# First weight pieces halved, first piece on ScalarE's queue, two x parts split on VectorE, other warm-up sizes

## The chip, the cores and the metric

The kernel runs on one core of a Trainium2 chip. Its time is the device time of one execution in microseconds; lower is better. Five engines work side by side, each through its own list of instructions in order: TensorE (PE, matmuls), VectorE (DVE), ScalarE (ACT), GpSimd (POOL) and SyncE (SP, which here only issues DMA transfers). ScalarE and GpSimd can issue transfers too.

## The reference

Two transformer blocks in a row on one sequence of 256 tokens of width 1024, all in float32. The part that matters here is the very beginning of the first block:

```python
xn = rms_norm(x, norm1_w[l])
z = xn @ w_in[l]
(q, k_c, v_c, k_s, v_s, k_w, v_w, g_nsa, xr, gr, g_a, g_b) = jnp.split(z, IN_SPLITS, axis=-1)
# rms_norm: xf * rsqrt(mean(xf * xf) + EPS) * w
```

After it come sparse attention with compressed keys, a gated linear recurrence (its decay uses `softplus(-lam)`), a merge, an MLP, and a second block with gated feed-forward layers and two more kinds of attention. All of that is matmuls with weights that are read once from memory, some 170 MB in all.

## The kernel before, in words

Precision: each float32 operand is split into a high part in TensorE's faster float32 format and a low part, the rest. A product takes three matmuls (high x high, high x low, low x high; `mmx`, L296 to L300). A weight piece is split by ScalarE (high: a copy, L248) and VectorE (low: a subtraction, L249). The activations of a norm are split in the same way by `split2` (L325 to L333), multiplied there by the norm's weight; the norm's 1/rms per token is applied later, when a product is taken out of PSUM.

Weights: `Plan` packs the weight blocks of all steps, in the order of the steps, into pieces. The first four pieces have 512 columns (256 KB), all others up to 1024 (512 KB). The first six pieces are loaded one by one (`chunks`, `load_to`), the later ones two to a transfer. The first `EARLY` transfers take tiles of the pool of 12 large buffers, the later ones three tiles of their own. `split_to` splits pieces two ahead of the one that is wanted, into five buffers for the high and five for the low parts.

The start: `setup` (L428) writes a tile of ones, runs three float32 matmuls on it as a warm-up (six passes in the profile, tile `hot`), loads the table for the sigmoid, and issues the first loads: the vector of small weights (`vec`, 56 KB) from ScalarE's queue, and from SyncE's queue x parts 0 to 1, weight piece 0, x parts 2 to 4, piece 1, x parts 5 to 7, piece 2. Then it splits the eight parts of x (tile `u`), high on ScalarE (L332), low on VectorE (L333).

The first projection is `kcvc` (step kv0, `fm1`): eight parts k of x by 256 columns, two blocks of three matmuls for each k, 48 matmuls of 256 columns. So pieces 0 to 3 hold k = 0 and 1, 2 and 3, 4 and 5, 6 and 7. The projection q0 follows (pieces 4 and 5), then xr0, k0, q1, xr1. Step `norm` (`norm0`, L542) squares x on ScalarE (L550), ordered behind the high part of piece 5, adds the squares on VectorE, and runs a short chain for 1/rms: sums on TensorE (L495), VectorE (L466), a power on GpSimd (tile `rs_A`, L468), a broadcast by TensorE (tile `bc_A`, L502), ScalarE (`rb_A`, L504). The evacuations of kcvc, q, xr and k multiply by `rb_A`.

Step `prep` (`rnn_prep`, L881) works out softplus of the recurrence's lambda, on 8 columns: two small operations, two sigmoids on ScalarE, and then a long row of GpSimd operations (L890 to L904). Its result is used only in the recurrence, later.

Order: the steps are issued in the order written in `ORDER_1`, but a scheduler then lays down each engine's list from an estimated timeline: an engine takes, of the instructions that are ready by that estimate, the one issued first (or marked as of high priority, as the norm's chain is). So work of later steps moves ahead where an engine is idle in the estimate: `prep` is begun as soon as `vec` is there. `behind` adds an order between two instructions of one engine and no wait. A transfer waits before its issue until the one eight places before it has landed.

Of the kernel before, what the change touches and what calls it, by code (L numbers as in the profile page):

```python
# [8 lines left out]
F32 = mybir.dt.float32  # L9
F32R = mybir.dt.float32r  # L10
AF = mybir.ActivationFunctionType
ALU = mybir.AluOpType
AX = mybir.AxisListType

P = 128
# [5 lines left out]
EPS = 1e-6  # L21
LOW = -float(2.0 ** 100)
PIECE = 1024
EARLY = 6
WIDE = ("g", "g", "g", "s", "s", "o")


# [1 line left out]
class Plan:  # L29
# [6 lines left out]

    def add(self, key, name, rows, cols):
        w = sum(n for _, n in cols)
        room = PIECE if len(self.pieces) > 4 else PIECE // 2
        if self.fresh or not self.pieces or self.pieces[-1][0] + w > room:  # L40
            self.pieces.append([0, []])
            self.fresh = False
        p = self.pieces[-1]
        self.loc[key] = (len(self.pieces) - 1, p[0], w)
        p[1].append((name, rows, cols))
        p[0] += w
# [4 lines left out]
    def chunks(self):  # L51

        out, i, n = [], 0, len(self.pieces)
        while i < n:
            c = 1 if i < 6 else 2
            out.append(list(range(i, min(n, i + c))))
            i += c
        return out
# [130 lines left out]
class Prog:  # L189
# [15 lines left out]
    def prepare(self):  # L205
        self.chunks = self.plan.chunks()
        self.chunk_of = {}
        self.off = []
        o = 0
        for ci, ch in enumerate(self.chunks):  # L210
            w = sum(self.plan.pieces[i][0] for i in ch)
            self.off.append((o, w))
            o += P * w
            x = 0
            for i in ch:
                self.chunk_of[i] = (ci, x)
                x += self.plan.pieces[i][0]
        self.total = o
        self.raw = {}
        self.split = {}  # L220
        self.n_dma = 0
        self.n_split = 0
        self.hi_ins = []
        self.raw_ins = []

    def load_to(self, c):
        while self.n_dma <= min(c, len(self.chunks) - 1):
            ci = self.n_dma
            o, w = self.off[ci]
            pool = "big" if ci < EARLY else "raw"  # L230
            t = self.pools[pool].tile([P, 2 * PIECE], F32, tag=pool, name=f"raw{ci}")
            self.raw_ins.append(self.nc.sync.dma_start(out=t[:, :w], in_=self.d["ws"][o:o + P * w].rearrange("(p w) -> p w", p=P)))
            if ci:
                self.behind(*self.raw_ins[:-3:-1])
            self.raw[ci] = t
            self.n_dma += 1

    def split_to(self, i):
        nc = self.nc
        while self.n_split <= min(i, len(self.plan.pieces) - 1):  # L240
            p = self.n_split
            ci, x = self.chunk_of[p]
            self.load_to(ci + 2 if ci >= EARLY else max(ci + 2, EARLY))
            w = self.plan.pieces[p][0]
            src = self.raw[ci][:, x:x + w]
            hi = self.pools["whi"].tile([P, PIECE], F32R, tag="whi", name=f"whi{p}")
            lo = self.pools["wlo"].tile([P, PIECE], F32R, tag="wlo", name=f"wlo{p}")
            self.hi_ins.append(nc.scalar.activation(out=hi[:, :w], in_=src, func=AF.Copy))  # L248
            nc.vector.tensor_tensor(out=lo[:, :w], in0=src, in1=hi[:, :w].bitcast(F32), op=ALU.subtract)  # L249
            self.split[p] = (hi, lo)  # L250
            self.n_split += 1

# [122 lines left out]
def build(nc, tc, d, out, es, dbg=None):  # L375
# [22 lines left out]
    G = Prog(nc, tc, pools, d, dbg)  # L398
    one = pools["one"]
    V = {}  # L400
    S = {}

    def keep(name, shape, dt=F32):
        t = one.tile(list(shape), dt, tag=name, name=name)
        S[name] = t
        return t
# [21 lines left out]
    def setup():  # L428

        hot = G.tmp("hot")  # L430
        nc.vector.memset(hot, 1.0)
        hb = G.ps("t", "hot")
        for _ in range(3):
            nc.tensor.matmul(hb, hot[:, :P], hot, start=True, stop=True)
        warm = G.small((P, 1), "warm")
        nc.vector.memset(warm, 1.0)
        nc.scalar.activation(out=warm, in_=warm, func=AF.Sigmoid)
        ones = keep("ones", (P, 2))
        nc.vector.memset(ones, 1.0)
        nc.vector.memset(keep("mhalf", (P, 2)), -0.5)  # L440
        res = G.big("res")
        S["res"] = res
        vec = keep("vec", (P, NVEC))
        nc.scalar.dma_start(out=vec, in_=d["vec"])
        nc.sync.dma_start(out=res[:, 0:2, :], in_=d["x"][:, 0:2, :])
        G.load_to(0)
        nc.sync.dma_start(out=res[:, 2:5, :], in_=d["x"][:, 2:5, :])
        G.load_to(1)
        nc.sync.dma_start(out=res[:, 5:8, :], in_=d["x"][:, 5:8, :])
        G.load_to(2)  # L450
        vec2 = keep("vec2", (P, NVEC2))
        o = 0
        for k in _VEC:
            V[k] = vec[:, o:o + 8]
            o += 8
        V["pos"] = vec2[:, 0:32].rearrange("p (k j) -> p k j", k=2)
        V["w2k"] = vec2[:, 32:288].rearrange("p (h c) -> p h c", h=2)
        V["w2v"] = vec2[:, 288:416].rearrange("p (h c) -> p h c", h=2)
        S["u0"] = Parts(G.big, "u0")
        for k in range(8):  # L460
            G.split2(*S["u0"].tile(k), res[:, k, :], V["norm1"][:, k:k + 1])

    def rstd_of(ss, name, n=2, add=EPS):

        v = G.small((P, n), "v_" + name)
        nc.vector.tensor_scalar(out=v, in0=ss, scalar1=1.0 / D, scalar2=add, op0=ALU.mult, op1=ALU.add)  # L466
        r = G.small((P, n), "rs_" + name)
        nc.gpsimd.tensor_tensor(out=r, in0=v, in1=S["mhalf"][:, :n], op=ALU.pow)  # L468
        return r
# [60 lines left out]
    def norm_chain(v, name):  # L530
# [4 lines left out]
        S["rb" + name] = bcast(r, name)  # L535

    G.step(setup)


# [341 lines left out]
    def rnn_prep():  # L881

        pr = keep("rp", (P, 4, 8))
        cc, ta, tb, tc_ = (pr[:, i, :] for i in range(4))
        nc.gpsimd.tensor_scalar(out=ta, in0=V["lam"], scalar1=-1.0, scalar2=None, op0=ALU.mult)
        nc.vector.tensor_tensor(out=tb, in0=ta, in1=V["lam"], op=ALU.min)
        G.table("sigmoid", out=tc_, in_=tb, func=AF.Sigmoid, scale=-1.0)
        G.table("sigmoid", out=tb, in_=tb, func=AF.Sigmoid)
        nc.vector.reciprocal(tc_, tc_)
        nc.gpsimd.tensor_tensor(out=tb, in0=tb, in1=tc_, op=ALU.mult)  # L890
        w = G.small((P, 8), "sp_w")
        z = G.small((P, 8), "sp_z")
        z2 = G.small((P, 8), "sp_z2")
        nc.gpsimd.tensor_scalar(out=w, in0=tb, scalar1=2.0, scalar2=None, op0=ALU.add)
        nc.vector.reciprocal(z, w)
        nc.gpsimd.tensor_tensor(out=z, in0=z, in1=tb, op=ALU.mult)
        nc.gpsimd.tensor_tensor(out=z2, in0=z, in1=z, op=ALU.mult)
        nc.gpsimd.tensor_scalar(out=w, in0=z2, scalar1=1.0 / 19.0, scalar2=None, op0=ALU.mult)
        for k in (17, 15, 13, 11, 9, 7, 5, 3, 1):
            nc.gpsimd.tensor_scalar(out=w, in0=w, scalar1=1.0 / k, scalar2=None, op0=ALU.add)  # L900
            nc.gpsimd.tensor_tensor(out=w, in0=w, in1=z if k == 1 else z2, op=ALU.mult)
        nc.gpsimd.tensor_scalar(out=ta, in0=ta, scalar1=0.0, scalar2=-8.0, op0=ALU.max, op1=ALU.mult)
        nc.gpsimd.tensor_scalar(out=w, in0=w, scalar1=-16.0, scalar2=None, op0=ALU.mult)
        nc.gpsimd.tensor_tensor(out=cc, in0=w, in1=ta, op=ALU.add)  # L904
        S["cc"] = cc
# [83 lines left out]
    queue = []  # L989
# [43 lines left out]
    def merge(tag, wa, wb, ka, kb, xa, xb, rows_a, rows_b):  # L1033
# [19 lines left out]
        def branch(p, sfx):  # L1053
# [3 lines left out]
            if p in done:  # L1057
# [13 lines left out]
        "gb": lambda p: fm1("gb", 4376, p, gb), "cw": cmp_w1, "lru": lru, "scan": lambda p: G.step(lambda: rnn_scan(p)),  # L1071
        "ma": lambda p: m1(p, "a"), "mb": lambda p: m1(p, "b"), "at": lambda n: [take() for _ in range(n)]}
    STEPS_1 = {"norm": norm0, "kv_fin": kcvc_fin, "cst": set_consts, "prep": rnn_prep, "cmp_x": cmp_x, "cmp_hT": cmp_hT, "cmp_fin": cmp_fin, "cmp_w2": cmp_w2, "cmp_attn": cmp_attn,
               "exp": rnn_exp, "sqrt": rnn_sqrt, "bt": rnn_bt, "gelu": rnn_gelu}
    for w in ORDER_1.split():
# [506 lines left out]
```

## Time and profile before

| | us |
|---|---|
| median of 3 runs | 966.34 (966.12 to 968.51) |
| the profiled execution | 966.17 |
| its span, first to last instruction | 964.4 |
| TensorE busy / weight loads | 948.3 / 870.1 |
| VectorE busy | 728.4 |
| ScalarE busy | 585.0 |
| GpSimd busy | 42.0 |
| granted TensorE clock, mean | 0.996 of full |
| moved by DMA | 174.03 MB, 180 GB/s over the span |

A row of the timeline gives the start, the time, the engine, the line of the kernel, the operation, the tile written and the tiles read, and in brackets how long the engine had been idle before and what released it. Times are from the start of the span. A row of a stretch gives, for each engine, its busy time in it and the number of instructions, and at the end the granted TensorE clock, the busy share of the 16 DMA engines and GB/s. Matmuls are pipelined, so the durations of single ones overlap.

### The profile page before, as it was taken

To read this page: it belongs to the slowest core of one execution; us is meant where nothing else is said; L and a number is where in the kernel's file an instruction comes from. 1 tells how busy PE (TensorE), PEld (TensorE's weight loads), DVE (VectorE), ACT (ScalarE), POOL (GpSimd) and SP (SyncE) were. 2 spreads that over 40 slices of the span, in tenths; PEclk is the share of its full clock that TensorE was granted. 3 is DMA by queue.
4 is the path that set the end of the run, shared out by engine and by line. 5 is a ranking of instruction groups with operands and counts; after the bars stand their busy time and mean duration, and the time that the engine had idled before them with its cause. 6 is when DMAs were issued, how large, how long until landed. Compare 5 with 4: busy or idle time off the path is not lost.

```text
span 964.4 us, 15990 instructions
## 1 busy us (share of the span) xinstructions
PE 948.3 (98%) x6310; PEld 870.1 (90%) x6310; DVE 728.4 (76%) x1219; ACT 585.0 (61%) x961; POOL 42.0 (4%) x71
## 2 busy tenths in 40 slices
PE   8999999999999999999999999899999999999997
PEld 7989999998888888888888889899999888888897
DVE  7898879879888655679888657779767878777553
ACT  6795898546767544566555445678764565555441
POOL 6100000000000000030000200000000000000000
PEclk9999999999999999999999999999999999999999
DMA  9575442634545555565555755353334565555541
GB/s 331 188 268 212 138 154 104 245 131 178 215 175 193 201 177 196 195 207 180 203 187 182 240 180 177 136 204 108 113 132 172 178 201 204 185 175 183 186 141 45
DMA packets 26556, 174.03 MB, mean 180 GB/s; under 512 B 3313, under 2 KB 3569, under 8 KB 7281
## 3 DMA queue, kind: packets, MB, share of 16 engines
q1 hardware_dynamic: 24912, 169.80, 49.8%
q0 software_dynamic: 1136, 2.63, 1.4%
q8 instruction: 49, 0.80, 0.3%
q10 hardware_dynamic: 432, 0.58, 0.2%
q14 instruction: 27, 0.21, 0.1%
HBM read 171.43 MB, written 1.05 MB: 179 GB/s over the span
## 4 chain that ended last, share of the span: by engine, by line
PE 93%; ACT 4%; DVE 1%; issue 1%; DMA 0%; POOL 0%; POOLq 0%; ACTq 0%
PE f L306 17%; PE w L306 12%; PE f L307 9%; PE w L307 6%; PE ld L294 6%; PE ga L300 5%; PE fd L306 4%; PE gb L300 4%; PE wo L306 3%; PE m1b L300 2%; PE fd L307 2%; PE xr L300 2%; PE gr L300 2%; PE wo L307 2%; PE va L294 1%; PE ka L300 1%
## 5 line engine op out<-in xcount | busy, mean ns | idle before, releaser
L249 DVE TENSOR_TENSOR wlo<-raw,whi 128x1024 fp32r<-128x1024 f32 (+3 forms) x322 | 389.1, 1210 | 168.0 <-ACT whi L248 150.3
L248 ACT ACTIVATE whi<-raw 128x1024 fp32r<-128x1024 f32 (+3 forms) x322 | 335.7, 1047 | 285.6 <-PE w L306 64.2
L306 PE MATMUL f<-u,whi 128*128 128x512 f32 x704 | 246.7, 396 | 0.0
L307 PE MATMUL f<-u,wlo 128*128 128x256 f32 x704 | 196.5, 279 | 0.0
L306 PEld LDWEIGHTS f<-u,whi 128*128 128x128 f32 x704 | 132.0, 188 | 31.3
L307 PEld LDWEIGHTS f<-u,wlo 128*128 128x128 f32 x704 | 132.7, 188 | 0.1
L306 PE MATMUL w<-u,whi 128*128 128x512 f32 x256 | 88.8, 392 | 0.0
L306 PE MATMUL w<-hid,whi 128*128 128x512 f32 x256 | 88.8, 391 | 0.0
L307 PE MATMUL w<-hid,wlo 128*128 128x256 f32 x256 | 71.7, 280 | 0.0
L307 PE MATMUL w<-u,wlo 128*128 128x256 f32 x256 | 71.3, 280 | 0.0
L306 PE MATMUL fd<-f1h,whi 128*128 128x512 f32 x176 | 61.1, 394 | 0.0
L294 PE MATMUL ld<-whi,f2h 128*128 128x256 f32 (+1 forms) x264 | 59.0, 319 | 0.0
L306 PEld LDWEIGHTS w<-hid,whi 128*128 128x128 f32 x256 | 47.9, 187 | 10.5
L306 PEld LDWEIGHTS w<-u,whi 128*128 128x128 f32 x256 | 47.7, 187 | 10.3
L300 PE MATMUL ga<-u,whi 128*128 128x256 f32 x256 | 48.2, 284 | 1.1 <-ACT whi L248 1.1
L307 PE MATMUL fd<-f1h,wlo 128*128 128x256 f32 x176 | 48.8, 277 | 0.0
L307 PEld LDWEIGHTS w<-u,wlo 128*128 128x128 f32 x256 | 48.3, 189 | 0.2
L307 PEld LDWEIGHTS w<-hid,wlo 128*128 128x128 f32 x256 | 48.4, 189 | 0.0
L300 PE MATMUL gb<-u,whi 128*128 128x256 f32 x256 | 48.2, 284 | 0.0
L294 PEld LDWEIGHTS ld<-whi,f2h 128*128 128x128 f32 x264 | 44.0, 191 | 3.4
L306 PE MATMUL wo<-m,whi 128*128 128x512 f32 x128 | 44.3, 393 | 0.0
L294 PE MATMUL ld<-wlo,f2h 128*128 128x256 f32 (+1 forms) x132 | 42.1, 319 | 0.0
(533 smaller groups left out, 1924.5 us busy)
## 6 DMA issues: line engine op xcount, KB each, us to landing
raw<-in_ws_dram SPq DMA_DIRECT2D x150, 1024.0 KB, 4.8
raw<-in_ws_dram SPq DMA_DIRECT2D x3, 960.0 KB, 4.8
raw<-in_ws_dram SPq DMA_DIRECT2D x2, 992.0 KB, 4.9
nar<-in_rpb_dram POOLq DMA_DIRECT2D x16, 96.0 KB, 6.0
raw<-in_ws_dram SPq DMA_DIRECT2D x4, 256.0 KB, 6.4
raw<-in_ws_dram SPq DMA_DIRECT2D x2, 512.0 KB, 7.0
raw<-in_ws_dram SPq DMA_DIRECT2D x1, 932.0 KB, 5.1
res<-in_x_dram SPq DMA_DIRECT2D x2, 384.0 KB, 6.2
```

Source lines behind the costliest of these rows:

```text
L248: self.hi_ins.append(nc.scalar.activation(out=hi[:, :w], in_=src, func=AF.Copy))
L249: nc.vector.tensor_tensor(out=lo[:, :w], in0=src, in1=hi[:, :w].bitcast(F32), op=ALU.subtract)
L294: mm(out, a, b, start=start and r == 0, stop=stop and r == 2, skip_group_check=True)
L300: mm(out, a, b, start=start and r == 0, stop=stop and r == 2, skip_group_check=True)
L306: mm(bank.rearrange("p (a t) -> p a t", a=2), wh, x, start=start, stop=False, skip_group_check=True)
L307: mm(bank[:, :T], wl, x[:, 0, :], start=False, stop=stop, skip_group_check=True)
```

## The change

The first two pieces get 256 columns (k = 0, and k = 1), so that there are seven single pieces before the pairs, and `EARLY` is 7; from the third on, pieces hold the same blocks as before (k = 2 and 3 and so on). Piece 0 is issued from ScalarE's queue. `vec` goes to SyncE's queue, as its first. The rule that keeps loads in order starts with the third. The x parts 0 and 1 are split on VectorE alone. The warm-up gets a fourth matmul, of 256 columns. The squares are still ordered behind `hi_ins[5]`, which is now the high part of the first q piece, and the load of the identity behind `raw_ins[4]`, now the last kcvc piece. The minimum that begins the lambda chain on VectorE is ordered behind the low part of piece 6, the second q piece.

```diff
--- before.py
+++ after.py
@@ -21,7 +21,7 @@
 EPS = 1e-6
 LOW = -float(2.0 ** 100)
 PIECE = 1024
-EARLY = 6
+EARLY = 7
 WIDE = ("g", "g", "g", "s", "s", "o")
 
 
@@ -36,7 +36,7 @@
 
     def add(self, key, name, rows, cols):
         w = sum(n for _, n in cols)
-        room = PIECE if len(self.pieces) > 4 else PIECE // 2
+        room = PIECE if len(self.pieces) > 5 else PIECE // 2 if len(self.pieces) > 2 else PIECE // 4
         if self.fresh or not self.pieces or self.pieces[-1][0] + w > room:
             self.pieces.append([0, []])
             self.fresh = False
@@ -52,7 +52,7 @@
 
         out, i, n = [], 0, len(self.pieces)
         while i < n:
-            c = 1 if i < 6 else 2
+            c = 1 if i < EARLY else 2
             out.append(list(range(i, min(n, i + c))))
             i += c
         return out
@@ -221,6 +221,7 @@
         self.n_dma = 0
         self.n_split = 0
         self.hi_ins = []
+        self.lo_ins = []
         self.raw_ins = []
 
     def load_to(self, c):
@@ -229,8 +230,9 @@
             o, w = self.off[ci]
             pool = "big" if ci < EARLY else "raw"
             t = self.pools[pool].tile([P, 2 * PIECE], F32, tag=pool, name=f"raw{ci}")
-            self.raw_ins.append(self.nc.sync.dma_start(out=t[:, :w], in_=self.d["ws"][o:o + P * w].rearrange("(p w) -> p w", p=P)))
-            if ci:
+            queue = self.nc.sync if ci else self.nc.scalar
+            self.raw_ins.append(queue.dma_start(out=t[:, :w], in_=self.d["ws"][o:o + P * w].rearrange("(p w) -> p w", p=P)))
+            if ci > 1:
                 self.behind(*self.raw_ins[:-3:-1])
             self.raw[ci] = t
             self.n_dma += 1
@@ -246,7 +248,7 @@
             hi = self.pools["whi"].tile([P, PIECE], F32R, tag="whi", name=f"whi{p}")
             lo = self.pools["wlo"].tile([P, PIECE], F32R, tag="wlo", name=f"wlo{p}")
             self.hi_ins.append(nc.scalar.activation(out=hi[:, :w], in_=src, func=AF.Copy))
-            nc.vector.tensor_tensor(out=lo[:, :w], in0=src, in1=hi[:, :w].bitcast(F32), op=ALU.subtract)
+            self.lo_ins.append(nc.vector.tensor_tensor(out=lo[:, :w], in0=src, in1=hi[:, :w].bitcast(F32), op=ALU.subtract))
             self.split[p] = (hi, lo)
             self.n_split += 1
 
@@ -430,8 +432,8 @@
         hot = G.tmp("hot")
         nc.vector.memset(hot, 1.0)
         hb = G.ps("t", "hot")
-        for _ in range(3):
-            nc.tensor.matmul(hb, hot[:, :P], hot, start=True, stop=True)
+        for n in (512, 512, 512, 256):
+            nc.tensor.matmul(hb[:, :n], hot[:, :P], hot[:, :n], start=True, stop=True)
         warm = G.small((P, 1), "warm")
         nc.vector.memset(warm, 1.0)
         nc.scalar.activation(out=warm, in_=warm, func=AF.Sigmoid)
@@ -441,9 +443,9 @@
         res = G.big("res")
         S["res"] = res
         vec = keep("vec", (P, NVEC))
-        nc.scalar.dma_start(out=vec, in_=d["vec"])
+        nc.sync.dma_start(out=vec, in_=d["vec"])
+        G.load_to(0)
         nc.sync.dma_start(out=res[:, 0:2, :], in_=d["x"][:, 0:2, :])
-        G.load_to(0)
         nc.sync.dma_start(out=res[:, 2:5, :], in_=d["x"][:, 2:5, :])
         G.load_to(1)
         nc.sync.dma_start(out=res[:, 5:8, :], in_=d["x"][:, 5:8, :])
@@ -458,7 +460,13 @@
         V["w2v"] = vec2[:, 288:416].rearrange("p (h c) -> p h c", h=2)
         S["u0"] = Parts(G.big, "u0")
         for k in range(8):
-            G.split2(*S["u0"].tile(k), res[:, k, :], V["norm1"][:, k:k + 1])
+            h, l = S["u0"].tile(k)
+            w = V["norm1"][:, k:k + 1]
+            if k > 1:
+                G.split2(h, l, res[:, k, :], w)
+                continue
+            nc.vector.tensor_scalar(out=h, in0=res[:, k, :], scalar1=w, scalar2=None, op0=ALU.mult)
+            nc.vector.scalar_tensor_tensor(out=l, in0=res[:, k, :], scalar=w, in1=h.bitcast(F32), op0=ALU.mult, op1=ALU.subtract)
 
     def rstd_of(ss, name, n=2, add=EPS):
 
@@ -883,7 +891,7 @@
         pr = keep("rp", (P, 4, 8))
         cc, ta, tb, tc_ = (pr[:, i, :] for i in range(4))
         nc.gpsimd.tensor_scalar(out=ta, in0=V["lam"], scalar1=-1.0, scalar2=None, op0=ALU.mult)
-        nc.vector.tensor_tensor(out=tb, in0=ta, in1=V["lam"], op=ALU.min)
+        G.behind(nc.vector.tensor_tensor(out=tb, in0=ta, in1=V["lam"], op=ALU.min), G.lo_ins[6])
         G.table("sigmoid", out=tc_, in_=tb, func=AF.Sigmoid, scale=-1.0)
         G.table("sigmoid", out=tb, in_=tb, func=AF.Sigmoid)
         nc.vector.reciprocal(tc_, tc_)
```

## Rows read from the trace of the kernel before

**Rows 1.** The page, busy time of each engine (share of the span) and instructions.

```profile
PE 948.3 (98%) x6310; PEld 870.1 (90%) x6310; DVE 728.4 (76%) x1219; ACT 585.0 (61%) x961; POOL 42.0 (4%) x71
```

**Rows 2.** Stretches: us, busy time (instructions) per engine, clock, DMA share, GB/s.

```profile
1.46:5.75 4.29, 4.29 (x6) 1.67 (x6) 0.31 (x2) 1.20 (x2) 0.80 (x2) 1.00 0.80 138
...
4.60:5.90 1.30, 1.15 (x3) 0.19 (x1) 0.34 (x2) 0.09 (x1) 0.30 (x2) 1.00 0.48 45
...
5.75:7.38 1.63, 0.00 (x0) 0.00 (x0) 1.12 (x5) 1.57 (x5) 0.26 (x1) 1.00 0.93 360
7.38:12.14 4.76, 4.05 (x26) 3.35 (x26) 4.56 (x11) 4.41 (x11) 3.80 (x8) 1.00 1.04 411
...
22.00:44.00 22.00, 22.00 (x187) 22.00 (x186) 18.80 (x30) 12.89 (x20) 6.49 (x14) 1.00 0.68 242
44.00:50.00 6.00, 5.75 (x43) 4.89 (x42) 5.75 (x19) 5.88 (x14) 0.00 (x0) 1.00 0.00 0
...
56.00:60.00 4.00, 2.48 (x20) 2.04 (x19) 3.17 (x10) 4.00 (x13) 0.00 (x0) 1.00 0.89 305
```

**Rows 3.** The chain that ended last: start us, us, what.

```profile
12.14 2.90 PE kcvc L300 x22
15.04 5.76 PE q L300 x48
```

**Rows 4.** Timeline of SyncE's queue: when transfers are issued.

```profile
1.19 0.42 SPq L232 DMA_DIRECT2D raw<-in_ws_dram  x1
1.66 0.42 SPq L447 DMA_DIRECT2D res<-in_x_dram  x1
```

**Rows 5.** DMA issues of 1.0 to 2.0: KB each, us from issue to landing.

```profile
raw<-in_ws_dram SPq DMA_DIRECT2D x1, 256.0 KB, 4.5
...
res<-in_x_dram SPq DMA_DIRECT2D x1, 384.0 KB, 5.9
```

**Rows 6.** DMA queues in 4.0 to 4.6: packets, MB, share of 16 engines.

```profile
q0 software_dynamic: 10, 0.00, 159.9%
```

**Rows 7.** Timeline of ScalarE and VectorE, 5.8 to 14.8: the first splits.

```profile
5.81 0.21 ACT L268 ACTIVATE rp<-rp 128x8 f32<-128x8 f32 x1 [3.13 <-DVE rp L886]
...
5.92 0.89 ACT L332 ACTIVATE u<-res,vec 128x256 fp32r<-128x256 f32 x2
...
6.45 0.88 DVE L333 SCALAR_TENSOR_TENSOR u<-res,vec,u 128x256 fp32r<-128x256 f32 x2 [0.20 <-ACT u L332]
6.72 0.61 ACT L248 ACTIVATE whi<-raw 128x512 fp32r<-128x512 f32 x1
...
9.61 0.69 DVE L249 TENSOR_TENSOR wlo<-raw,whi 128x512 fp32r<-128x512 f32 x1
...
11.85 1.06 ACT L248 ACTIVATE whi<-raw 128x1024 fp32r<-128x1024 f32 x1 [0.21 <-DMA raw<-in_ws_dram]
...
12.95 2.58 DVE L249 TENSOR_TENSOR wlo<-raw,whi 128x1024 fp32r<-128x1024 f32 x2 [0.26 <-ACT whi L248]
...
14.18 0.62 ACT L550 ACTIVATE acc<-res 128x512 f32<-128x512 f32 x1
```

**Rows 8.** Timeline of the lambda chain and of the norm.

```profile
5.61 0.17 DVE L886 TENSOR_TENSOR rp<-rp,vec 128x8 f32<-128x8 f32 x1 [0.18 <-POOL rp L885]
...
9.03 0.33 POOL L896 TENSOR_TENSOR sp_z<-sp_z,rp 128x8 f32<-128x8 f32 x1 [0.32 <-DVE sp_z L895]
...
10.47 0.31 POOL L900 TENSOR_SCALAR sp_w<-sp_w 128x8 f32<-128x8 f32 x1
...
11.24 1.54 POOL L900 TENSOR_SCALAR sp_w<-sp_w 128x8 f32<-128x8 f32 x1
...
22.82 0.17 DVE L466 TENSOR_SCALAR v_A<-sscA 128x2 f32<-128x2 f32 x1
...
25.35 0.73 POOL L468 TENSOR_TENSOR rs_A<-v_A,mhalf 128x2 f32<-128x2 f32 x1
...
26.96 0.38 PE L502 MATMUL bc_A<-ident,rs_A 128*128 128x128 f32 x2
```

## The prediction

> **What bounds the kernel now.** Read first the busy shares of the page [rows 1]: TensorE is busy 948.3 of 964.4 us, so the most that any edit of order can give back is its idle 16.1 us. Next the stretches [rows 2]: the reader is to see that this change touches only the first 60 us, and that TensorE's idle there lies in four places. It does nothing for 1.63 us between its warm-up (ends 5.75) and the first projection matmul (7.38); from 7.38 to 12.14 it is busy 4.05 of 4.76; from 22 to 44 it never stops; in 44 to 50 it loses 0.25 and in 56 to 60 it loses 1.52, while ScalarE is full in both. Then the chain of waits [rows 3]: from 12.14 TensorE alone carries it, the last 22 of 48 kcvc matmuls end at 15.04, and the next 48 take 5.76, 0.12 each. At that pace kcvc needs 5.76 us, and it takes 15.04 - 7.38 = 7.66: it stalls 1.9 us.
>
> Why, the issues and the landings tell [rows 4, 5]: the first weight piece, second on SyncE's queue, is issued at 1.19 and takes 4.5, so lands at 5.69; x parts 2 to 4 are issued at 1.66, take 5.9 and land only at 7.56. The stretch 4.60 to 5.90 shows the pause: 45 GB/s, against 411 in 7.38 to 12.14 [rows 2]. In 4.0 to 4.6 ten packets of the software queue hold 159.9% of 16 engines' time, that is 1.5 us each [rows 6]; the only such transfer then in flight is the sink row. So I read the pause as engines held by it. From 5.9 the transfers run without a gap: the early part is bound by the order of bytes, and the first q piece (512 KB) ends ScalarE's wait only at 11.85 [rows 7].
>
> **The change, part by part.**
>
> *Head of the queues.* SyncE issues vec, x 0 to 1, x 2 to 4 where it issued x 0 to 1, piece 0, x 2 to 4, so the third issue stays at 1.66. ScalarE issues piece 0 in place of vec: one for one. x 0 to 1 takes the second place, whose 256 KB landed at 5.69. The vec of 56 KB ahead of it is smaller than the 256 KB that stood there, so 5.69 is a late estimate.
>
> *First two x parts on VectorE.* ScalarE loses 0.89 us for two [rows 7], VectorE gains two tensor_scalar on 128x256, a form not shown: between 0.17 (the tiny one of v_A [rows 8]) and 0.44 (half of 0.88, two inputs, same tile [rows 7]); I take 0.44, the nearer tile. High part ready at 5.69 + 0.44 = 6.13, low part at 6.57. ScalarE also no longer stands behind the lambda sigmoid at 5.81.
>
> *Warm-up.* Six passes take 4.29 [rows 2], 0.715 each; two more of half size add 0.72 and end at 6.47. It becomes the last to end before the first matmul (6.13 for the operand). The start moves from 7.38 to about 6.5, but k = 0 has only six matmuls now (0.72), done at 7.2.
>
> *Order of the pieces.* This is what decides. Piece 1 (k = 1) now comes after x 2 to 4, and k = 2 and 3, which came right after x 2 to 4, now come after x 5 to 7. Behind x 2 to 4 (7.56) stand 128 + 384 + 256 KB, 786 kB at 411 GB/s: 1.91 us, so k = 2 and 3 land at 9.47. High part 0.61, low part 0.69 [rows 7]: 10.08 and 10.77; the measured low part of the same columns ended at 9.61 + 0.69 = 10.30. From 10.77 there are 10 + 24 matmuls left of kcvc, 4.08 us, if nothing more is late: end 14.85 against 15.04. A second stall, the wait that ended at 12.14, should go, as VectorE starts some 0.3 us earlier (6.13 against 6.45) and has no reciprocals and minimum between. If the pause lets as many bytes through ahead of it as now, x 2 to 4 lands 128 KB = 0.32 us earlier and the end is 14.53. So the front gives 0.2 to 0.5; I take 0.3. Ends of this term: a loss of 0.45 if the short rows of the two 128 KB pieces cost as much engine time as long ones (twice 0.32 later, less 0.19); above, the first q piece caps it: 11.85 + 1.06 + 1.29 (half of 2.58) = 14.20, needed at 15.04 + 0.24, slack about 1.0; if the 1.3 us pause went too, 1.16 more, 2.2 in all. The extra issue and extra split instructions are covered: transfers are backlogged until 11.85.
>
> *Squares.* They now follow the first q piece's high part, not the second's. Four of about 0.6 (the first 0.62 at 14.18 [rows 7]) may come before the second q piece's high part: that ends at 12.91 + 2.4 + 1.06 = 16.4 and its low part at 17.6; TensorE wants it at 14.74 + 2.88 + 0.24 = 17.86. Free, by 0.3.
>
> *Lambda chain moved behind the second q piece's low part.* Now GpSimd goes through it from 9.03 and without a break into rs_A at 25.35 [rows 8]: 23 operations in 16.3 us, 0.71 each, and rs_A has waited since v_A at 22.82 + 0.17. TensorE is not hurt, since bc_A stands only at 26.96. In the changed kernel the chain starts later; where rs_A is put among it is the scheduler's choice. If rs_A goes first, it runs 2.4 us earlier or more, and the evacuations of q, kcvc and xr that wait for it move into ScalarE's idle 9.1 us of 22 to 44. That relieves ScalarE in 44 to 60, where TensorE loses 1.77. Bounds: 0 to 1.77 gained; also below nothing, the third rival. I take half, 0.9, as weight conversions and the exp table load there stay.
>
> A rule that speaks against this move: the same L900 operation on 8 columns takes 0.31 at 10.47 and 1.54 at 11.24, when VectorE is converting weights [rows 8]. The Trainium skill, SBUF — State Buffer, "Who interferes with whom", says that a VectorE instruction with two SBUF inputs and a GpSimd instruction that reads SBUF shut each other out of a shared port. The trace agrees in kind, 1.54 against 0.31.
>
> *Rest.* The seventh early tile needs 1 + 7 + 2 of the 12 large buffers, so nothing waits. Pieces from the first q piece on are the same.
>
> **Sum.** 0.3 + 0.9 = 1.2 off the profiled run's own 966.17 (span 964.4 and 1.8 around it; 0.17 below the median 966.34): 965.0.
>
> **The rivals.**
>
> *More: both places give nearly all* (chance 0.2). The pause shrinks because the second queue is at work, front 1.0 to 2.2, and the middle gives 1.77: 2.8 to 4.0, so 962.2 to 963.4. For: the pause lies exactly where a third issue of SyncE waits, and its cause is inferred. Against: the sink row is issued as before, and the k = 2 and 3 weights move back.
>
> *Nothing* (0.2). The order of bytes gives back what the early start wins, and ScalarE's full stretch stays: 966.2, between 965.6 and 966.9. For: 411 GB/s with no gap. Also here: the change does not do what it says, since k = 1 arrives after k = 0 is finished and the earlier start is only an earlier stall.
>
> *Slower: GpSimd is in the way of the norm* (0.2). If the scheduler lays n operations of the lambda chain before rs_A, TensorE stands at bc_A. The chain can start only after 12.95 + 2.58 = 15.53; from the minimum to the first of the 23 operations passed 9.03 - 5.61 = 3.4, so it starts at 18.9 or later. rs_A ends at 18.9 + 0.71 n + 0.73, bc_A is reached at about 26.7: it decides from n = 10. With n = 16, TensorE waits 4.3 us: 966.2 - 0.3 + 4.3 = 970.2; with all 23, 9.3 us: 975. Small overruns, n = 11 to 13, give 966.6 to 968. For: today all of it lies before rs_A. Against: rs_A has the higher priority and the chain starts 10 us later. By the skill's rule the operations would be the slow kind, and n = 6 at 1.54 would do; that is one reason for a chance of 0.2.
>
> **How the numbers follow.** The forecast has 0.4 (964 to 966 is its own range). Differences within 0.3%, 2.9 us, are about what a measurement of this kernel can't tell from none: faster is below 963.4, slower above 969.2. Faster: half of the first rival and some of the forecast's upper end and of orders later on that fall out better, 0.17. Slower: more than half of the third rival, 0.13. Same: 0.7. The range reaches over most of the first rival and the small overruns of the third: 962.7 to 968.5.
>
> **What would show it.** First kcvc matmul at 6.5, right behind the warm-up, then a gap of about 1 us before k = 1 and another before k = 2, whose conversion starts as its load lands (about 9.5); kcvc ends at 14.5 to 14.9. rs_A directly behind v_A, and less idle in 44 to 60. Wrong if x 2 to 4 lands well before 7.2 (the pause was not the sink row), if TensorE waits at bc_A for rs_A, or if the stretches after 60 us differ by more than 1 us.

## The result, and the profile after

The changed kernel is slower: 972.93 us, median of 4 runs (972.29 to 974.85), against 966.93 (966.12 to 968.51) for the kernel before beside it, ratio 1.0066 (95% interval 1.0053 to 1.0079). The forecast was 965.0, its range ended at 968.5. The profiled execution took 973.46 (span 971.7), 7.3 more than the one before. From line 234 on, the changed kernel's line numbers are 2 higher than those ahead of the prediction, in the later functions 8 higher.

The page of the changed kernel, against [rows 1]: TensorE's busy time has *grown* by 3.0, though the work is the same but for one warm-up matmul. The longer warm-up makes 1.4 of it (5.67 busy against 4.29). A busy time that grows by more than that says that something ran slower, not only later.

```profile
PE 951.3 (98%) x6312; PEld 873.3 (90%) x6312; DVE 729.8 (75%) x1222; ACT 586.7 (60%) x962; POOL 38.4 (4%) x71
```

Stretches of the changed kernel (columns as in [rows 2]):

```profile
7.38:12.14 4.76, 2.23 (x13) 1.41 (x12) 3.58 (x9) 4.14 (x10) 0.00 (x0) 1.00 1.04 412
44.00:50.00 6.00, 5.88 (x50) 5.62 (x49) 5.91 (x15) 5.88 (x11) 0.00 (x0) 1.00 0.03 12
56.00:60.00 4.00, 4.00 (x35) 3.96 (x33) 4.00 (x10) 4.00 (x13) 0.00 (x0) 1.00 0.86 303
60.00:80.00 20.00, 18.73 (x154) 18.14 (x153) 19.23 (x37) 14.22 (x24) 3.24 (x4) 1.00 0.81 302
0.00:60.00 60.00, 54.80 (x405) 50.54 (x405) 48.30 (x99) 44.00 (x81) 17.07 (x39) 1.00 0.70 248
0.00:150.00 150.00, 143.53 (x1140) 138.43 (x1141) 126.89 (x275) 114.16 (x212) 20.32 (x43) 1.00 0.59 210
150.00:170.00 20.00, 16.75 (x112) 16.10 (x110) 17.98 (x40) 14.57 (x20) 0.00 (x0) 0.83 0.30 106
160.60:166.60 6.00, 5.94 (x26) 5.75 (x27) 6.00 (x11) 3.00 (x6) 0.00 (x0) 0.50 0.52 178
```

and of the kernel before, those that the prediction did not show:

```profile
60.00:80.00 20.00, 19.88 (x164) 19.45 (x164) 19.59 (x39) 14.68 (x22) 3.23 (x4) 1.00 0.77 273
0.00:60.00 60.00, 54.43 (x403) 49.80 (x404) 49.50 (x100) 45.06 (x83) 20.66 (x39) 1.00 0.73 259
0.00:150.00 150.00, 144.11 (x1143) 138.50 (x1144) 127.01 (x271) 116.75 (x215) 23.89 (x43) 1.00 0.59 210
150.00:170.00 20.00, 20.00 (x166) 19.78 (x165) 20.00 (x46) 15.76 (x32) 0.00 (x0) 1.00 0.30 106
```

In 150 to 170 the changed kernel does 112 matmuls where the one before did 166: 54 x 0.12 = 6.5 us behind, nearly all of the loss, at a place that no line of the diff names. The early stretches give and take: 7.38 to 12.14 lost 1.8 of TensorE's time, 40 to 60 shows 1.2 of idle in place of 1.8, 60 to 80 has 1.27 in place of 0.12. Without the passes of the warm-up (8, and 6 before) both kernels have 397 matmuls behind them at 60, and at 150 the changed one has 1132 against 1137: all that comes before 150 makes five matmuls, about 0.6 us. What TensorE waits for, changed kernel (us in total, times, longest):

```profile
PE ka L302 <- DVE qa L1263: 3.3, 1, 3.3
PE o L877 <- ACT pt101h L331: 3.3, 1, 3.3
PE kcvc L302 <- ACT whi L250: 2.3, 2, 1.8
...
PE cmph L681 <- ACT whi L250: 1.3, 1, 1.3
PE vg L296 <- DVE wlo L251: 1.1, 1, 1.1
```

The first stands in both kernels. The second is new. (The kernel before has kcvc 1.6, `ga` 1.1 and cmph 0.4 for `whi`, and nothing for vg.) TensorE around it, in the changed kernel:

```profile
157.00 0.40 PE L302 MATMUL gb<-u,whi 128*128 128x256 f32 x2
160.66 1.22 PE L877 MATMUL o<-pt101h,v 128*128 128x512 f32 x2 [3.25 <-ACT pt101h L331]
...
161.89 0.63 PE L302 MATMUL gb<-u,whi 128*128 128x256 f32 x2
```

It stands 3.25 us for `pt101h`, the high part of one block of transposed attention weights. Then the same form that took 0.40 takes 0.63, for 6 us: the granted clock is 0.50 (1.2 GHz) in 160.6 to 166.6, where 26 matmuls fit and at full pace 50 would: 24 x 0.12 = 2.9. The wait and the half clock make 6.15 of the 6.5. Behind 166.6 the clock is whole again: the form takes 0.40 at 167.13. Why `pt101h` was late stands in ScalarE's timeline. Kernel before:

```profile
141.20 1.28 ACT L268 ACT_TABLE_LOAD   x1
142.49 1.06 ACT L268 ACTIVATE rt<-rt 128x1024 f32<-128x1024 f32 x1
...
144.40 1.04 ACT L268 ACTIVATE rt<-rt 128x1024 f32<-128x1024 f32 x1
145.46 1.28 ACT L268 ACT_TABLE_LOAD   x1
146.76 2.01 ACT L268 ACTIVATE rg<-rg 128x1024 f32<-128x1024 f32 x2
148.67 0.47 ACT L329 ACTIVATE pt100h<-ptn 128x384 fp32r<-128x384 f32 x1
149.04 0.48 ACT L329 ACTIVATE pt101h<-ptn 128x384 fp32r<-128x384 f32 x1
...
151.57 0.63 ACT L985 ACTIVATE tgb<-tgb 128x512 f32<-128x512 f32 x1
```

and the matmul there that reads `pt101h`:

```profile
155.26 0.63 PE L869 MATMUL o<-pt101h,v 128*128 128x512 f32 x2
```

Changed kernel:

```profile
141.82 1.28 ACT L270 ACT_TABLE_LOAD   x1
143.12 1.06 ACT L270 ACTIVATE rt<-rt 128x1024 f32<-128x1024 f32 x1
...
146.87 0.48 ACT L331 ACTIVATE pt100h<-ptn 128x384 fp32r<-128x384 f32 x1
147.37 1.28 ACT L993 ACT_TABLE_LOAD   x1
148.66 0.63 ACT L993 ACTIVATE tgb<-tgb 128x512 f32<-128x512 f32 x1
...
150.26 1.28 ACT L270 ACT_TABLE_LOAD   x1
151.56 1.06 ACT L270 ACTIVATE rt<-rt 128x1024 f32<-128x1024 f32 x1
152.63 1.28 ACT L270 ACT_TABLE_LOAD   x1
153.93 2.01 ACT L270 ACTIVATE rg<-rg 128x1024 f32<-128x1024 f32 x2
155.95 1.28 ACT L270 ACT_TABLE_LOAD   x1
...
158.25 1.99 ACT L250 ACTIVATE whi<-raw 128x1024 fp32r<-128x1024 f32 x2
160.14 0.47 ACT L331 ACTIVATE pt101h<-ptn 128x384 fp32r<-128x384 f32 x1
```

Read the tiles from top to bottom (`rt` is the square root, `rg` the gelu, `tgb` the tanh). Before: sqrt, sqrt, gelu, tanh with two table loads, and `pt101h` next to `pt100h`. It was ready at 149.52, and TensorE read it 5.7 us later. Changed: sqrt, *tanh*, sqrt, gelu, each behind a load of its own, so 12 table loads in the kernel in place of 10. All of it, a further load, two exponentials and two weight splits stand ahead of `pt101h`, which comes 11.1 us later, more than that slack. No instruction here was edited; the scheduler laid ScalarE's list in another order from its estimated timeline. It could, because the kernel issues its square roots, gelus and exponentials through `table`, which orders one group behind the other, and this tanh without it.

The Trainium skill, ScalarE: Activation LUTs, "What ACT_TABLE_LOAD costs", gives 1283 ns for the load and 2.66 us with a drain for each switch. Here the loads take 1.28, start 0.01 to 0.02 behind the instruction ahead (146.87 + 0.48, then 147.37), and the next one starts 0.01 to 0.02 behind them (141.82 + 1.28, then 143.12): no drain shows, and the two more cost 2.6 in all on ScalarE. The greater price is what waits behind them.

### The profile page after: what moved, and what is told of

It reads as the page before. It is cut to its first block, busy times and chain, and to the rows that moved or that the text cites. A ratio compares the mean times of both kernels' runs of the same rounds, so it can differ in the third digit from the quotient of the medians.

```text
span 971.7 us, 16000 instructions
## 1 busy us (share of the span) xinstructions
PE 951.3 (98%) x6312; PEld 873.3 (90%) x6312; DVE 729.8 (75%) x1222; ACT 586.7 (60%) x962; POOL 38.4 (4%) x71
## 4 chain that ended last, share of the span: by engine, by line
PE 89%; ACT 5%; DVE 2%; POOL 1%; DMA 1%; issue 1%; SPq 0%; POOLq 0%; DVEq 0%; ACTq 0%
PE f L308 17%; PE w L308 12%; PE f L309 8%; PE w L309 6%; PE ld L296 6%; PE ga L302 5%; PE fd L308 4%; PE gb L302 3%; PE wo L308 3%; PE m1b L302 2%; PE fd L309 2%; PE gr L302 2%; ACT whi L250 2%; PE wo L309 2%; PE va L296 1%; PE ka L302 1%
## 5 line engine op out<-in xcount | busy, mean ns | idle before, releaser
L250 ACT ACTIVATE whi<-raw 128x1024 fp32r<-128x1024 f32 (+4 forms) x323 | 335.9, 1045 | 297.3 <-PE w L308 64.0
L251 DVE TENSOR_TENSOR wlo<-raw,whi 128x1024 fp32r<-128x1024 f32 (+4 forms) x323 | 389.0, 1207 | 165.7 <-ACT whi L250 148.3
```

Of the source, the lines that this page charges most:

```text
L251: self.lo_ins.append(nc.vector.tensor_tensor(out=lo[:, :w], in0=src, in1=hi[:, :w].bitcast(F32), op=ALU.subtract))
```

## The experiments

Theory T: most of the loss is that order at 141 to 160, its wait and the half clock behind it, and any small shift of the estimate can flip it. Rival G: the lambda chain on GpSimd, and what it holds up. Rival F: the front, late operands of kcvc. The kernel before, beside each set, measured 966.2 to 966.3; its own runs lie between 964.6 and 968.8, with a mean granted clock of 0.999 to 0.992, so medians and their intervals are compared, not single runs. What a trace shows is said of the one profiled execution.

**1. Undo one edit, and do one alone.** All of the change but the moved lambda chain:

```diff
-        G.behind(nc.vector.tensor_tensor(out=tb, in0=ta, in1=V["lam"], op=ALU.min), G.lo_ins[6])
+        nc.vector.tensor_tensor(out=tb, in0=ta, in1=V["lam"], op=ALU.min)
```

> All edits but the order of the lambda chain behind the second q piece. Its list of ScalarE around the two sqrt is that of the kernel before (10 table loads, not 12). Theory T, the loss lies at 141 to 160 us in ScalarE's list (a tanh between the two sqrt, two table loads more, TensorE waits 3.25 us, then 5.9 us at the lower clock) and some 1 us in the first 20 us: 966.9 to 968.3, no wait at 157. Rival G, the GpSimd chain ahead of the kcvc evacuation's loads makes the loss: also about 967, so this run alone doesn't tell them apart. Rival F, the start with small pieces makes all of it: 972 to 973.

Measured: 968.16 (ratio 1.0018, 1.0007 to 1.003), no wait for `pt101h`. (Its profiled execution, 970.99, is the slowest of its eleven: the granted clock fell to 0.50 in 13 to 15 and again in 64 to 66.) All of the change but the small pieces (`EARLY` is 6 again, and the chain stands behind `lo_ins[5]`, again the second q piece):

```diff
-        room = PIECE if len(self.pieces) > 5 else PIECE // 2 if len(self.pieces) > 2 else PIECE // 4
+        room = PIECE if len(self.pieces) > 4 else PIECE // 2
```

> All edits but the pieces of 256 columns (first piece on ScalarE's queue, x parts on VectorE, warm-up, lambda chain late). TensorE's order is that of the kernel before. T: 965.5 to 967.5, as the order at 141 to 160 is the old one. G: 971 to 973, as the GpSimd chain is still late. F: at or below 966.9.

Measured: 967.64 (1.0005, 0.9995 to 1.0016), no wait for `pt101h`. That is 0.1 above T's range and far below G's. The same edit the other way, the small pieces alone in the kernel before:

```diff
-EARLY = 6
+EARLY = 7
...
-        room = PIECE if len(self.pieces) > 4 else PIECE // 2
+        room = PIECE if len(self.pieces) > 5 else PIECE // 2 if len(self.pieces) > 2 else PIECE // 4
```

> The pieces of 256 columns alone, all other edits undone. ScalarE's list around the two sqrt is that of the changed kernel, 12 table loads. T: 972 to 974 with a wait of about 3 us at 157 and a stretch at the lower clock behind it. G: 966 to 968, since the lambda chain is early. F: 972 or more, with the loss in the first 20 us and none at 157.

Measured: 967.8 (1.0015, 1.0005 to 1.0025). The expectation named an order that this kernel does not have: its trace shows the old one, with `pt101h` right behind `pt100h` and no wait for it. So it doesn't test T; it prices the small pieces, at about 1.5 us, with the granted clock at 0.57 in 11 to 15 and q at 17.22. Undoing either edit takes away 5 of the 6 us, so neither owns them; all three kernels have the old order.

**2. The order alone.** All of the change, and one order: the first tanh behind the last gelu.

```diff
-            G.table("gelu", out=S["rg"][:, sl, :], in_=S["rg"][:, sl, :], func=AF.Gelu_apprx_tanh)
+            S["gelu_ins"] = G.table("gelu", out=S["rg"][:, sl, :], in_=S["rg"][:, sl, :], func=AF.Gelu_apprx_tanh)
...
-            nc.scalar.activation(out=t, in_=t, func=AF.Tanh, scale=0.5)
+            ins = nc.scalar.activation(out=t, in_=t, func=AF.Tanh, scale=0.5)
+            if key == "tgb" and p == 0:
+                G.behind(ins, S["gelu_ins"])
```

> All edits, and the first tanh of the gate gb ordered behind the last gelu, so that ScalarE loads 10 tables, not 12. T: the wait at 157 shrinks from 3.25 by about 2.6 us, to under 1 us; if the clock then stays up, 967 to 968, if it falls all the same, 970. G and F: 972 to 973, no change.

Measured: 969.12 (1.0022, 1.0011 to 1.0032), that is 3.8 less than the change, though above the 967 to 968 that T gave for a clock that stays up. No wait for `pt101h`, 10 table loads, and 150 to 170 is whole again:

```profile
150.00:170.00 20.00, 20.00 (x162) 19.54 (x161) 20.00 (x43) 17.03 (x35) 0.00 (x0) 1.00 0.38 116
```

Up to 150 TensorE has done what it does in the changed kernel, 1140 matmuls in both, so the gain lies behind that: the order is the larger part, as T says. The rest, 2 to 3 over the kernel before, lies early only in part (kcvc waits 2.1 for `whi`, cmph 1.2, vg 1.1): TensorE is 5 matmuls behind the kernel before at 150, 8 at 600 and 17 at 700. Between those two lies the wait at `ka`, behind which the granted clock stays at 0.50 from 614 to 620; in the kernel before, only in 616 to 618.

**3. The smallest edit.** All of the change but the fourth warm-up matmul, 256 columns:

```diff
-        for n in (512, 512, 512, 256):
+        for n in (512, 512, 512):
```

> All of the change but the fourth warm-up matmul. Theory T (most of the loss is an order of ScalarE's list at 141 to 160, with a tanh between the two square roots, which any small shift of the estimated timeline can flip): without that matmul the scheduler lays the old order down, 10 table loads, pt101h next to pt100h. So TensorE has no wait of 3 us at o, the granted clock stays 1.00 in 140 to 180, and the time is 967 to 969.5 against 972.9 of the full change, which is 3.5 to 6 us for the company of a matmul of 0.7 us. Rival G (the late lambda chain on GpSimd and the late compression loads cost most): those are all still there, 971 or more. Rival F (the front: late operands of kcvc): still there and longer by the 0.7 us that the warm-up no longer covers, 972 or more.

Measured: 970.06 (1.0035, 1.0023 to 1.0048): old order, no wait for `pt101h`, but above T's 967 to 969.5. By 150 it is 17 matmuls behind the kernel before, 2.0 us, and that begins at the front: TensorE ends its warm-up earlier, stands longer for k = 1, and then runs at half clock. Its wait there, and a stretch behind:

```profile
9.75 0.50 PE L302 MATMUL kcvc<-u,whi 128*128 128x256 f32 x2 [2.75 <-ACT whi L250]
```

```profile
13.00:15.00 2.00, 2.00 (x12) 2.00 (x12) 1.50 (x3) 2.00 (x4) 0.00 (x0) 0.56 1.06 440
```

So F was right on the place of a part, and wrong on the size. Most of the rest comes behind `ka`, where the clock stays at 0.50 from 616 to 622. Now the same matmul from the other side, without small pieces and without the moved chain: the kernel before with `vec` on SyncE's queue, piece 0 on ScalarE's, and the fourth warm-up matmul.

```diff
+            queue = self.nc.sync if ci else self.nc.scalar
...
+            if ci > 1:
...
-        for _ in range(3):
-            nc.tensor.matmul(hb, hot[:, :P], hot, start=True, stop=True)
+        for n in (512, 512, 512, 256):
+            nc.tensor.matmul(hb[:, :n], hot[:, :P], hot[:, :n], start=True, stop=True)
...
-        nc.scalar.dma_start(out=vec, in_=d["vec"])
+        nc.sync.dma_start(out=vec, in_=d["vec"])
+        G.load_to(0)
         nc.sync.dma_start(out=res[:, 0:2, :], in_=d["x"][:, 0:2, :])
-        G.load_to(0)
```

> The kernel before with two edits alone: vec on SyncE's queue and piece 0 on ScalarE's, and the fourth warm-up matmul. First pieces of 512 columns, x split as before, lambda chain early as before. By the scheduler this one has the new order of ScalarE's list (12 table loads). Theory T: TensorE waits 2.5 to 3.5 us at the first o matmul near 158 for pt101h, the granted clock then falls to half for some us, and the time is 970 to 972.5. Rivals G and F: neither the small pieces nor the moved lambda chain is there, so 965.5 to 968.

Measured: 973.08 (1.0066, 1.0053 to 1.0079), above T's 972.5, and the whole loss of the change. TensorE at 158, and the stretch:

```profile
160.49 1.22 PE L877 MATMUL o<-pt101h,v 128*128 128x512 f32 x2 [3.26 <-ACT pt101h L331]
```

```profile
150.00:170.00 20.00, 16.74 (x112) 16.09 (x111) 17.97 (x40) 14.40 (x20) 0.00 (x0) 0.83 0.29 106
```

The same without that matmul, the two queues alone:

```diff
-        for n in (512, 512, 512, 256):
+        for n in (512, 512, 512):
```

> The kernel before with one edit: vec on SyncE's queue and piece 0 on ScalarE's. It is the kernel that measured 973.08 without its fourth warm-up matmul of 256 columns (0.7 us of work for TensorE). By the scheduler it has the old order at 141 to 160. Theory T: no 3 us wait at o, clock 1.00 in 140 to 180, time 965.3 to 966.8, that is 6 to 8 us less than with that matmul. Rival: the changed queues themselves cost, 968 or more.

Measured: 966.92 (1.0011, 1.0 to 1.0022), old order, no wait for `pt101h`; 0.1 above T's upper end. One warm-up matmul of 256 columns is 6.2 us of time here. The front can't be the cause: q starts at 14.65 in the kernel of 973.08 and at 15.04 in this one. Nor can anything else ahead of 150: there the one has done 1134 matmuls without the warm-up, the other 1137. T stands; G and F are excluded for the main loss, since the kernel of 973.08 has neither the moved chain nor the small pieces.

**4. The pause, and the order of the bytes.** The kernel before, with the sink row's load late (`S["kvd"]` is the first load of `kv_sb`):

```diff
-        nc.gpsimd.dma_start(out=sk, in_=d["rows"][0, 0:8].partition_broadcast(P))
+        G.behind(nc.gpsimd.dma_start(out=sk, in_=d["rows"][0, 0:8].partition_broadcast(P)), S["kvd"])
```

> The kernel before with one order added: the load of the sink row (GpSimd's queue, one row to all partitions) stands behind the first load of kv_sb, so it is issued near 30 us and not in the first 4 us. My prediction read the pause of the transfers at 4.6 to 5.9 as engines held by that row. If so (theory S): no pause, over 300 GB/s in 4.6 to 5.9, x parts 2 to 4 land near 6.3 (7.56 before), kcvc starts 1.0 earlier for k of 2 and more, and the time is 965.0 to 966.0. If the pause has another cause (rival N): the rate in 4.6 to 5.9 stays below 150 GB/s, x 2 to 4 land after 7.2, time 966 to 967.5. The order of ScalarE's list at 141 to 160 is that of before in both.

Measured: 965.91 (0.9996, 0.9988 to 1.0005). The stretch of the pause:

```profile
4.60:5.90 1.30, 1.30 (x3) 0.34 (x1) 0.54 (x3) 0.46 (x2) 0.51 (x2) 1.00 1.00 379
```

379 GB/s against 45 [rows 2], and x parts 2 to 4 land at 1.65 + 4.7 = 6.35: the pause was the sink row. But q starts at 14.36 against 14.88, 0.52 and not 1.0 earlier, and of the time no gain can be told.

The change without the moved chain, piece 1 ahead of x parts 2 to 4, piece 2 ahead of x parts 5 to 7, sink row late (only the order of the loads is shown):

```diff
+        G.load_to(1)
         nc.sync.dma_start(out=res[:, 2:5, :], in_=d["x"][:, 2:5, :])
-        G.load_to(1)
+        G.load_to(2)
         nc.sync.dma_start(out=res[:, 5:8, :], in_=d["x"][:, 5:8, :])
-        G.load_to(2)
```

> All of the change but the moved lambda chain, and two things more: in SyncE's queue piece 1 (k = 1) goes ahead of x parts 2 to 4 and piece 2 (k = 2 and 3) ahead of x parts 5 to 7, and the sink row's load goes behind the first kv_sb load. Old order of ScalarE's list at 141 to 160. Theory: the front's loss of the changed kernel came from the late landing of k = 1 and of k = 2 and 3; with them ahead, kcvc starts near 6.8, q starts at 14.0 to 14.9 (16.28 in the changed kernel, 14.88 before), and the time is 965 to 966.5. Rival: x 2 to 4 land so much later, behind 128 KB more, that TensorE waits for u of k = 2 as long as it waited for the weights: q starts at 15.5 or later, 967 to 968.5.

Measured: 965.02 (0.9986, 0.9977 to 0.9994), q at 14.47. With the sink row left early:

```diff
-        G.behind(nc.gpsimd.dma_start(out=sk, in_=d["rows"][0, 0:8].partition_broadcast(P)), S["kvd"])
+        nc.gpsimd.dma_start(out=sk, in_=d["rows"][0, 0:8].partition_broadcast(P))
```

> The kernel with pieces 1 and 2 ahead of the x parts (965.02), with the sink row's load left where it was. If the sink row is worth what it was in the kernel before (kcvc ended 0.5 earlier without it): the pause at 4.6 to 5.9 is back, q starts 0.4 to 0.8 later than 14.47, time 965.3 to 966.3. If the order of the pieces gave all of the gain: 964.8 to 965.3.

Measured: 966.14 (1.0002, 0.9993 to 1.0011), q at 15.31. Against the 968.16 of the same kernel with the pieces in the change's order, that order is worth 2.0: it gives back what the change lost at the front, no more; the sink row late adds 1.1. The cheapest of all, the kernel before with the two queues changed (piece 0 on ScalarE's, as above) and the sink row late:

```diff
-        nc.scalar.dma_start(out=vec, in_=d["vec"])
+        nc.sync.dma_start(out=vec, in_=d["vec"])
+        G.load_to(0)
         nc.sync.dma_start(out=res[:, 0:2, :], in_=d["x"][:, 0:2, :])
-        G.load_to(0)
...
+        G.behind(nc.gpsimd.dma_start(out=sk, in_=d["rows"][0, 0:8].partition_broadcast(P)), S["kvd"])
```

> The kernel before with the two cheap things: vec on SyncE's and piece 0 on ScalarE's queue, and the sink row late. Pieces of 512 columns, old warm-up, old lambda chain, old order at 141 to 160. If the small pieces are of no use: q starts at 14.1 to 14.5, time 964.8 to 965.8, no worse than the 965.02 with small pieces. If the small pieces help: 966 or more.

Measured: 965.33 (0.9982, 0.9972 to 0.9992), q at 14.18, the earliest. The small pieces show no gain that can be told. Both versions beat the kernel before by 0.14 to 0.18%, a gain of 0.9 to 1.2 us in the medians.

## Why the prediction was wrong

**The sum stopped at 60 us: the step that failed.** The prediction opened with "this change touches only the first 60 us" and summed two terms from there. The description of the kernel itself says why that can't be taken as given: the lists are laid down from one estimated timeline, so a warm-up matmul can move every later decision. The term left out was -6.5 us. It even stood among the signs ("if the stretches after 60 us differ by more than 1 us") and got no price and no chance of its own; "orders later on that fall out better" were counted, those that fall out worse were not. The price could have been bounded from the traces of before: TensorE already stands 3.3 us once, at `ka` near 612, and the granted clock falls to 0.65 in 616 to 620. The two terms that were summed, +1.2 together, came out at nothing by 60 (397 matmuls in both kernels) and at about -0.6 by 150; for the first 60 us that is what the rival *Nothing* said.

**The front: +0.3 forecast, -1.4 measured where q starts** (16.28 against 14.88); by 60 it is made good, as 40 to 60 has 153 matmuls against 141. The first matmul came at 6.78 (6.5 forecast), and the sign named for this step, a gap before k = 1 and another before k = 2, is there. ScalarE and TensorE in the changed kernel:

```profile
8.00 1.31 ACT L334 ACTIVATE u<-res,vec 128x256 fp32r<-128x256 f32 x3 [4.34 <-DMA res<-in_x_dram]
9.21 0.40 ACT L250 ACTIVATE whi<-raw 128x256 fp32r<-128x256 f32 x1
9.52 1.29 ACT L334 ACTIVATE u<-res,vec 128x256 fp32r<-128x256 f32 x3
10.72 1.66 ACT L250 ACTIVATE whi<-raw 128x512 fp32r<-128x512 f32 x3
```

```profile
6.78 0.59 PE L302 MATMUL kcvc<-u,whi 128*128 128x256 f32 x2
...
9.67 0.50 PE L302 MATMUL kcvc<-u,whi 128*128 128x256 f32 x2 [1.83 <-ACT whi L250]
...
11.38 0.51 PE L302 MATMUL kcvc<-u,whi 128*128 128x256 f32 x2 [0.43 <-ACT whi L250]
```

Two mis-sized pieces. First, x parts 2 to 4 landed at 7.9 (the chain of waits has 1.65 + 6.26), not 7.56 or earlier, and k = 2 and 3 at 9.97 (3.07 + 6.9), not 9.47. The pause came earlier: 21 GB/s in 3.5 to 4.6, where the kernel before had 227, and 136 in 4.6 to 5.9. Why it moved stays open. Second, the forecast counted landings and the time of the splits but not ScalarE's order: piece 1 had landed by about 8.3, yet three `u` splits (1.31) stood ahead of its high part (9.21), and three more ahead of that of k = 2 (10.72, forecast to be *finished* at 10.08). The "loss of 0.45" taken as the lower end was too small by 1.

**The middle: +0.9 forecast.** It supposed rs_A 2.4 us or more earlier, "if rs_A goes first". It did not: five of the 23 operations went ahead, and it ran at 26.10 (25.35 before). TensorE did not stand at bc_A, but the slower rival's n = 10 was not the bound either: the first of the 23 began at 22.93, not at 18.9, and bc_A came at 28.23, not at 26.7, so that by the rival's own sum 22.93 + 0.71 n + 0.73 it would have decided from n = 7. What nobody priced is what else GpSimd issues. The rest of the chain, changed kernel:

```profile
26.10 0.73 POOL L476 TENSOR_TENSOR rs_A<-v_A,mhalf 128x2 f32<-128x2 f32 x1
...
34.22 0.28 POOL L909 TENSOR_TENSOR sp_w<-sp_w,sp_z 128x8 f32<-128x8 f32 x1
34.45 0.64 POOL L576 DMA_DIRECT2D cmpA<-kv_sb  x1
...
36.20 0.60 POOL L577 DMA_DIRECT2D cmpA<-kv_sb  x1
```

The four loads of the compression's operand are issued at 34.45 to 36.2; the kernel before issued them at 29.39 to 31.14. Of these 5.06, 1.28 are `kv_sb` itself, ready at 30.36 in place of 29.08. The last takes 5.5 to land, and VectorE stands 1.81 for it at 41.84. The idle of 44 to 50 and 56 to 60 did shrink, from 1.77 to 0.12, but vg waits 1.09 at 51.30, so over 40 to 60 it went only from 1.76 to 1.22. In 60 to 80 cmph waits 1.26 at 62.46 (0.41 at 58.33 before), and 1.15 more is lost than before. How much of that the late loads own is not shown: without the moved chain cmph still waits 1.04, and vg 0.18. Without this edit the change measured 968.16, with the lists in the old order.

**The pause: right** that the sink row makes it (379 against 45 GB/s without the row), and on x 2 to 4 not landing before 7.2 with it. How the row makes it is not shown: the prediction read it from packets of 1.5 us each, but in the changed kernel the row's packets in 4.0 to 4.6 are four and hold 8.1% of the engines' time, and the rate there is still 32 GB/s.

## What to carry to other kernels

Where a scheduler lays the lists from an estimate, an edit's cost is not local: compare every engine's order before and after over the whole kernel before summing, and give "the order flips elsewhere" a price and a chance. Bind the orders that matter (here: both square roots, then gelu, then tanh) with a written order, so that tuning one end does not reroll the other. Before a chain is moved on an engine, list everything that engine also issues: here four transfers of GpSimd went out 5 us later, while TensorE never waited for the norm on the same engine.

## What was not expected of the hardware

The clock falls for rather short stops, and not for all: to 0.50 after a stop of 3.25 (here at 160.66) and in 62 to 64 of the kernel with 973.08 after one of 1.55 that ended at 60.80, behind a stretch (58 to 60) that was busy 1.24 of 2; after 2.75 to 0.56 in 13 to 15 with the fourth warm-up matmul left out; after 2.11 to 0.50 in 13 to 15 without the moved chain; after 1.92 to 0.57 in 11 to 15 with the small pieces alone; but not after the 1.83 of the changed kernel at 9.67. What parts them stays open. And one row of 8 numbers sent to all partitions through the software queue, 4 KB in all, all but stops the other queues: a rate of 45 GB/s in 4.6 to 5.9 that is 379 without it.
